# Rotating images by 90 degrees: all loads first, then all stores, on one DMA queue

## The chip, the core and the metric

The kernel runs on one core of a Trainium2 chip. The metric is device time in microseconds (us), the median of several executions. All runs that are compared are on record as fast, with a granted clock of 1.00. Of each kernel one run was profiled.

Some words used below. HBM is the chip's large memory, SBUF the core's own memory of 128 partitions; DMA transfers move data between them, on 16 DMA engines. A transfer has landed when each of its 16 shares has added its step to the transfer's semaphore (the counter that others wait for). An instruction fetch is a packet of the profile's instruction queue (q14).

## The reference

The input is `x` of shape (32, 3, 256, 256) in fp32, 25.17 MB. The output is as large:

```python
def reference(x):
    return np.rot90(x, k=-1, axes=(-2, -1)).astype(np.float32)
```

No arithmetic is done. 25.17 MB must come in from HBM and 25.17 MB must go out.

## The kernel before

The data are cut into 24 slabs of 1 MB. A slab is 128 partitions of 8 rows of 256 numbers, so 8 KB per partition, contiguous in HBM. VectorE's 32x32 transpose, with reversed access patterns, does the rotation. A slab is loaded on the queue of the sync engine (SP), transposed in two halves, and stored on the queue of the scalar engine (ACT).

```python
in_pool = ctx.enter_context(tc.tile_pool(name="in_pool", bufs=12))
out_pool = ctx.enter_context(tc.tile_pool(name="out_pool", bufs=12))
for n in range(n_slabs):                       # 24
    t_in = in_pool.tile([P, R * W], fp32, tag="t_in")      # R = 8, W = 256
    nc.sync.dma_start(out=t_in, in_=ld_v[n])
    t_out = out_pool.tile([P, R * W], fp32, tag="t_out")
    src = t_in.rearrange("p (r g c) -> p c r g", r=R, c=R)
    dst = t_out.rearrange("p (c g r) -> p c r g", c=R, r=R)[:, :, ::-1, ::-1]
    for k in range(PARTS):                     # PARTS = 2
        cs = slice(k * CP, (k + 1) * CP)       # CP = 4
        nc.vector.transpose(out=dst[:, cs], in_=src[:, cs])
    nc.scalar.dma_start(out=st_v[n], in_=t_out,
                        max_dma_last_dim=2048 if n < SHORT else 8192)   # SHORT = 2
# ... (shapes, views and the launch are cut)
```

The first two stores are issued in packets of 2 KB instead of 8 KB.

## Time and profile before

| | before |
|---|---|
| time, median of 6 runs | 124.47 us (124.41 to 124.64) |
| span of the profiled run | 122.8 us |
| VectorE busy | 92.5 us |
| bytes moved | 50.33 MB |

From the page of the kernel before: the busy time of VectorE (DVE); the strip of 40 equal slices with the DMA engines' busy share in tenths and what they moved; the two data queues (packets, MB, share of 16 engines' time); the chain of waits by engine; and VectorE's group.

```profile
span 122.8 us, 186 instructions
...
DVE 92.5 (75%) x48; POOL 0.2 (0%) x4
...
DMA  3999999999999999999999999999999999999993
GB/s 93 422 427 427 393 427 422 415 420 432 426 408 411 427 427 427 427 427 427 427 427 430 427 427 427 427 427 430 427 430 427 427 427 430 424 427 427 427 430 163
...
q1 hardware_dynamic: 3456, 25.17, 49.3%
q10 hardware_dynamic: 4224, 25.17, 48.9%
...
DMA 72%; DVE 8%; DVEq 2%; SPq 1%; issue 0%
...
L54 DVE STREAM_TRANSPOSE t_out<-t_in 128x1024 f32<-128x1024 f32 x48 | 92.5, 2047 | 9.7 <-DMA t_in<-in_x_dram 7.9
```

The DMA strip is full from the second slice to the last but one. VectorE has a quarter of the span to spare. The kernel is bound by the DMA engines.

The table of stretches of the kernel before. The columns are the stretch, its length, the busy time of VectorE and GpSimd with their instruction counts, the clock, the DMA engines' busy share (just over 1 where packets overlap a little), and GB/s.

```profile
core 0: us, DVE busy (x) POOL busy (x), PEclk, DMA share, GB/s
3.00:12.00 9.00, 6.45 (x4) 0.00 (x0) 1.00 1.01 425
12.00:38.00 26.00, 26.00 (x14) 0.00 (x0) 1.00 1.02 417
38.00:62.00 24.00, 24.00 (x14) 0.00 (x0) 1.00 1.01 427
...
64.00:120.00 56.00, 34.09 (x18) 0.00 (x0) 1.00 1.01 427
```

At 3 to 12 us only loads run, from 38 to 97 us loads and stores are mixed, after 98 us only stores are left. The rate to compare with is 427 GB/s. What is below it lies at the start and at 12 to 38 us, in two dips of the rate near 12 and 36 us. A stretch counts a packet where it starts, so up to 16 packets of 8 KB can fall on either side of an edge: over 9 us that is 15 GB/s, over 24 us 5 GB/s. Differences of a few GB/s are safe only in the long stretches.

### The profile page before, as it was taken

The numbers are of one execution on the slowest core, as the hardware profiler recorded it, in microseconds if no ns is written. First come the engines' busy times: TensorE is split into PE (matmuls) and PEld (weight loads), VectorE is DVE, ScalarE is ACT, GpSimd is POOL, SyncE is SP. The second block draws the span as 40 slices with busy tenths as digits, with TensorE's granted clock in tenths as the row PEclk, the third lists the DMA queues.
The fourth block names the chain that finished last, engine by engine and source line by source line (L and its number), as shares of the span: only waits on it lengthen the run. The fifth ranks groups of instructions, "written<-read, shape, count | busy, mean of one in ns | idle before, by whom it ended". The sixth has DMA issues, their size and how long they took to land.

```text
span 122.8 us, 186 instructions
## 1 busy us (share of the span) xinstructions
DVE 92.5 (75%) x48; POOL 0.2 (0%) x4
## 2 busy tenths in 40 slices
DVE  0199999999999999999999999897796693000000
POOL 0000000000000000000000000000000000000000
DMA  3999999999999999999999999999999999999993
GB/s 93 422 427 427 393 427 422 415 420 432 426 408 411 427 427 427 427 427 427 427 427 430 427 427 427 427 427 430 427 430 427 427 427 430 424 427 427 427 430 163
DMA packets 7681, 50.34 MB, mean 410 GB/s; under 512 B 768, under 2 KB 768, under 8 KB 1792
## 3 DMA queue, kind: packets, MB, share of 16 engines
q1 hardware_dynamic: 3456, 25.17, 49.3%
q10 hardware_dynamic: 4224, 25.17, 48.9%
q14 instruction: 1, 0.01, 0.0%
HBM read 25.17 MB, written 25.17 MB: 410 GB/s over the span
## 4 chain that ended last, share of the span: by engine, by line
DMA 72%; DVE 8%; DVEq 2%; SPq 1%; issue 0%
DMA t_in<-in_x_dram 72%; DVE t_out L54 8%; DVEq L83 2%; SPq L47 1%; DVEq L54 0%
## 5 line engine op out<-in xcount | busy, mean ns | idle before, releaser
L54 DVE STREAM_TRANSPOSE t_out<-t_in 128x1024 f32<-128x1024 f32 x48 | 92.5, 2047 | 9.7 <-DMA t_in<-in_x_dram 7.9
L72 POOL MEMSET const-bfloat16-1.0<- 128x1 bf16 x1 | 0.1, 101 | 0.0
L72 POOL MEMSET const-uint8-127<- 128x1 uint8 x1 | 0.1, 101 | 0.0
L72 POOL MEMSET const-float32-0.0<- 128x1 f32 x1 | 0.1, 98 | 0.2 <-issue 0.2
L72 POOL MEMSET const-float32-1.0<- 128x1 f32 x1 | 0.1, 98 | 0.0
## 6 DMA issues: line engine op xcount, KB each, us to landing
t_in<-in_x_dram SPq DMA_DIRECT2D x24, 1024.0 KB, 14.5
out_dram<-t_out ACTq DMA_DIRECT2D x24, 1024.0 KB, 19.5
```

The source lines that it names most:

```text
L47: nc.sync.dma_start(out=t_in, in_=ld_v[n])
L54: nc.vector.transpose(out=dst[:, cs], in_=src[:, cs])
L72: nc = _bacc.Bacc("TRN2", target_bir_lowering=False, num_devices=1)
L83: with _tile.TileContext(nc) as tc:
```

## The change

All loads are issued first, then all stores, and all on SP's queue. With 25 units of 8 KB per partition no load ever waits for a buffer: slab n is transposed into the unit that slab n-1 left, and slab 0 into the spare one. The short rows go. The first store is cut into its first row (1 KB per partition) and the rest.

```diff
-    in_pool = ctx.enter_context(tc.tile_pool(name="in_pool", bufs=12))
-    out_pool = ctx.enter_context(tc.tile_pool(name="out_pool", bufs=12))
+    pools = [ctx.enter_context(tc.tile_pool(name=f"unit{u}", bufs=1)) for u in range(N_UNITS)]
+    units = [p.tile([P, R * W], fp32, name=f"u{u}") for u, p in enumerate(pools)]
     for n in range(n_slabs):
-        t_in = in_pool.tile([P, R * W], fp32, tag="t_in")
-        nc.sync.dma_start(out=t_in, in_=ld_v[n])
+        nc.sync.dma_start(out=units[n], in_=ld_v[n])
-        t_out = out_pool.tile([P, R * W], fp32, tag="t_out")
+    for n in range(n_slabs):
+        t_in, t_out = units[n], units[n - 1]
         # ... the two transposes, the same
-        nc.scalar.dma_start(out=st_v[n], in_=t_out,
-                            max_dma_last_dim=2048 if n < SHORT else 8192)
+        cuts = [0, W, R * W] if n == 0 else [0, R * W]
+        for a, b in zip(cuts, cuts[1:]):
+            nc.sync.dma_start(out=st_v[n][:, a:b], in_=t_out[:, a:b])
```

The intent is a stream of DMA work in which nothing waits for a buffer, with one turn from reading HBM to writing it.

More of the change, by code (lines that the diff above doesn't have):

```diff
@@ L34 @@
     n_slabs = B * C * G // P
-    PARTS = 2
-    SHORT = 2
-    CP = R // PARTS
+    N_UNITS = n_slabs + 1
     ld_v = x.rearrange("b c h w -> (b c h) w").rearrange("(n p r) w -> n p (r w)", p=P, r=R)
     st_v = out.rearrange("b c h w -> (b c h) w").rearrange("(n p c) w -> n p (c w)", p=P, c=R)
-    in_pool = ctx.enter_context(tc.tile_pool(name="in_pool", bufs=12))
-    out_pool = ctx.enter_context(tc.tile_pool(name="out_pool", bufs=12))
+    pools = [ctx.enter_context(tc.tile_pool(name=f"unit{u}", bufs=1)) for u in range(N_UNITS)]
+    units = [p.tile([P, R * W], fp32, name=f"u{u}") for u, p in enumerate(pools)]
     for n in range(n_slabs):
-        t_in = in_pool.tile([P, R * W], fp32, tag="t_in")
-        nc.sync.dma_start(out=t_in, in_=ld_v[n])
-        t_out = out_pool.tile([P, R * W], fp32, tag="t_out")
+        nc.sync.dma_start(out=units[n], in_=ld_v[n])
+    for n in range(n_slabs):
+        t_in, t_out = units[n], units[n - 1]
         src = t_in.rearrange("p (r g c) -> p c r g", r=R, c=R)
         dst = t_out.rearrange("p (c g r) -> p c r g", c=R, r=R)[:, :, ::-1, ::-1]
-        for k in range(PARTS):
-            cs = slice(k * CP, (k + 1) * CP)
+        for h in range(2):
+            cs = slice(h * R // 2, (h + 1) * R // 2)
             nc.vector.transpose(out=dst[:, cs], in_=src[:, cs])
-        nc.scalar.dma_start(out=st_v[n], in_=t_out,
-                            max_dma_last_dim=2048 if n < SHORT else 8192)
+        cuts = [0, W, R * W] if n == 0 else [0, R * W]
+        for a, b in zip(cuts, cuts[1:]):
+            nc.sync.dma_start(out=st_v[n][:, a:b], in_=t_out[:, a:b])
 _INS = ['x']
```

## The prediction

> **What bounds the kernel now.** The DMA engines. It moves 25.17 MB in and 25.17 MB out; the utilisation strip has DMA at nine tenths in every slice but the first and last, and the table of stretches gives 427 GB/s from 38 to 97 us, where loads and stores mix. VectorE is busy 92.5 us of 122.8; the chain of waits is 72% DMA. At 427 GB/s, 50.33 MB take 117.9 us (estimate). The other 4.9 us are, from the same table and the DMA packets: about 2.5 us before the engines run full, about 0.6 us lost between 12 and 38 us (393, 421 and 396 GB/s instead of 427), and about 1.8 us at the end (unequal engines to 121.65 us, then 1.2 us to the end of the span).
>
> **What the change does.**
> 1. Loads and stores no longer mix. This should cost and gain nothing: loads alone run at 425 GB/s (3 to 12 us), the mix at 427, stores alone at 426 (98 to 120 us). The Trainium skill, "DMA: Bandwidth & Descriptors", section "Issuing engines are not separate DMA queues", says that transfers issued by different engines run on the same 16 DMA engines and interleave; the trace agrees.
> 2. The two 2 KB-row stores go. A 2 KB packet took 84 ns, four of them 336 ns, against 309 ns for one 8 KB packet. Two stores are 64 small packets per engine: about 0.4 us. With the dips at 12 and 36 us that is the 0.6 us. A first row of 128 packets of 1 KB is added: under 0.1 us (estimate by the same fixed part per packet).
> 3. One turn from reading to writing, near 61 us. Estimate from the two dips of before: 0.1 to 0.3 us lost.
> 4. Startup and ending are the same.
> 5. The transposes are the same 48, 2.04 us each. No load reuses a unit, so no load waits for VectorE. Slab j is transposed near 5.6 + 3.86(j+1) us, the last at about 98. On the one queue its store can start only after all loads and j stores, at about 61 + 2.46 j us, the last at about 117.6. VectorE is over 15 us ahead everywhere. Stores are issued in order, each also waiting for the transfer eight places earlier; with eight transfers of 2.46 us in flight the engines don't starve.
>
> So only items 2 and 3 lie on the critical path: -0.6 + 0.1 + 0.2 us.
>
> **Prediction.** 124.0 us, 8 in 10 between 123.3 and 125.0. Faster by over 2%: 0.02; within 2%: 0.95; slower by over 2%: 0.03.
>
> **What the profile would show.** Span near 122.3 us. DMA strip full throughout, near 427 GB/s in nearly every slice; one queue, last load landing near 61 us, stores only afterwards, one small dip there. VectorE busy unchanged at 92.5 us, idle from about 98 us to the end for lack of work. The chain of waits almost wholly DMA.
>
> **What would make it wrong.** Reading alone might not hold 425 GB/s for 59 us (before shows only 9 us of it): 4% less would cost 2.4 us. A single queue might drain at the turn, when the stores' first packets wait for the loads' last ones: a bubble of 1 to 2 us. The engines may end more unevenly. The other way, the gain might reach 1 us; more is not there to have.

## The result, and the profile after

The changed kernel took 124.61 us (median of 6, 124.49 to 124.67) against 124.47 us before. A ratio here is always the mean time of one kernel's runs over the mean of the other's in the same rounds, so it is not quite the ratio of the quoted medians. It is 1.0008, with a 95% interval of 0.9995 to 1.0021. The two kernels are equally fast, and the half microsecond that the prediction expected did not come.

The page of the kernel after, the same lines:

```profile
span 122.9 us, 190 instructions
...
DVE 95.6 (78%) x48; POOL 0.2 (0%) x4
...
DMA  3999999999999999999999999999999999999993
GB/s 83 416 427 429 429 424 421 427 427 419 413 419 427 427 421 421 424 424 413 424 414 429 427 429 427 429 429 427 421 427 427 427 429 427 427 427 427 427 435 165
...
q1 hardware_dynamic: 7056, 50.33, 98.0%
q14 instruction: 2, 0.02, 0.0%
...
DVE 43%; issue 34%; DMA 4%; DVEq 2%
...
L53 DVE STREAM_TRANSPOSE u<-u 128x1024 f32<-128x1024 f32 x48 | 95.6, 2057 | 6.4 <-DMA u<-in_x_dram 5.6
```

Two readings need care. First, the chain of waits now names VectorE for 43% and "issue" for 34%. That is not what bounds the kernel. VectorE's last transpose ended at 102.0 us, while the last store landed at 122.05 us; the DMA strip is as full as before. The chain lost the DMA queue because every store here was issued long before its data moved. Second, VectorE's 95.6 us are not slower transposes (2057 ns against 2047 ns). Before, successive transposes overlapped a little, one slab per 3.81 us where nothing else was waited for; now they follow at one slab per 4.02 us, each slab also waiting for VectorE's own previous one. Neither matters.

What the issuing engine waited for, from the view of waits of the kernel after (SPq is SP's sequencer; total us, times, longest us):

```profile
SPq L45 <- DMA u<-in_x_dram: 32.9, 16, 2.2
SPq L57 <- DMA out_dram<-u: 32.7, 17, 2.4
...
SPq L57 <- DMA u<-in_x_dram: 16.7, 8, 2.1
...
SPq L57 <- DVE u L53: 0.6, 2, 0.3
```

Stores hardly ever waited for VectorE (0.6 us). They waited for earlier transfers, as the design wants.

The table of stretches of the kernel after, the same columns:

```profile
3.00:12.00 9.00, 6.32 (x4) 0.00 (x0) 1.00 1.00 422
12.00:38.00 26.00, 25.76 (x14) 0.00 (x0) 1.00 1.01 423
38.00:62.00 24.00, 23.79 (x13) 0.00 (x0) 1.00 1.01 421
...
64.00:120.00 56.00, 37.71 (x19) 0.00 (x0) 1.00 1.01 427
```

At 38 to 62 us before had the mix at 427 GB/s; after has loads alone at 421. From 64 us on, with stores alone, it is back at 427. Between 12 and 38 us after is a little faster than before, and loads alone again.

A finer account comes from the DMA packets of the two traces. For each moment, the time elapsed minus the bytes moved so far divided by 427.5 GB/s is the time lost up to then. Its increase by stretch, in us:

| stretch | before | after | what happens there |
|---|---|---|---|
| 0 to 12 us | 2.61 | 2.70 | start, loads only |
| 12 to 17 | 0.25 | 0.00 | before: the stores begin |
| 17 to 36 | 0.19 | 0.24 | before: 2 KB packets; after: loads only |
| 36 to 38 | 0.22 | 0.02 | before: the stores' packets become 8 KB |
| 38 to 62 | 0.00 | 0.32 | before: the mix; after: loads only |
| 62 to 64 | 0.00 | 0.07 | after: the turn |
| 64 to 121 | 0.10 | 0.05 | |
| sum | 3.37 | 3.40 | |

Before loses 0.66 us from 12 to 38 us, and the change removes nearly all of it. After loses 0.58 us in the loads, all of it from 17 us on, and 0.07 us at the turn. Removing and adding cancel.

How a run of loads loses time shows in the landings (the increments of each transfer's semaphore; the first of its 16) beside the packets:

| after | packets of load done, first engine | landed, first share | lag |
|---|---|---|---|
| load 0 | 5.04 us | 5.38 us | 0.34 us |
| load 3 | 12.41 | 12.81 | 0.40 |
| load 5 | 17.31 | 17.78 | 0.47 |
| load 14 | 39.67 | 40.15 | 0.48 |
| load 23 | 62.02 | 62.50 | 0.48 |

From load 5 to load 23 the landings come every 44.72 / 18 = 2.484 us. Stores 2 to 23 land every (121.31 - 69.82) / 21 = 2.452 us. The packets of the first five loads ran at 2.454 us each, faster than they landed, until they were 0.47 us ahead. Then they were held to the landing rate: 8 KB packets of 309 ns became packets of up to some 321 ns. So the 425 GB/s that the prediction read off the first 9 us of before was the rate of the packets while they ran ahead. The landings of before said otherwise already: loads 0 to 3 landed at 5.23, 7.70, 10.20 and 12.68 us, 2.483 us apart.

### The profile page after: what moved, and what is told of

Same layout as the page of the kernel before. It is cut to its first block, busy times and chain, and to the rows that moved or that the text cites. A ratio compares the mean times of both kernels' runs of the same rounds, so it can differ in the third digit from the quotient of the medians.

```text
span 122.9 us, 190 instructions
## 1 busy us (share of the span) xinstructions
DVE 95.6 (78%) x48; POOL 0.2 (0%) x4
## 4 chain that ended last, share of the span: by engine, by line
DVE 43%; issue 34%; DMA 4%; DVEq 2%
DVE u L53 43%; DMA u<-in_x_dram 4%; DVEq L83 2%
## 5 line engine op out<-in xcount | busy, mean ns | idle before, releaser
L53 DVE STREAM_TRANSPOSE u<-u 128x1024 f32<-128x1024 f32 x48 | 95.6, 2057 | 6.4 <-DMA u<-in_x_dram 5.6
```

## The experiments

Runs of different submissions were on different chips, so they are compared by their ratio to the kernel before, which ran beside each. Two questions were put to the chip. Is the slow run of loads a property of loading, or does VectorE or the queue make it? And are the terms that the change removed (short rows, early turn, the cut row) worth what the reading says?

### e1: before without its short rows

```diff
-    SHORT = 2
+    SHORT = 0
```

> The kernel before with its first two stores in 8 KB rows too, nothing else changed. If the 2 KB rows and the turn that they bring cost what the prediction said, this is 0.4 to 0.6 us faster than before (about 124.0 us) and the load packets' dip at 36 us is gone. Rival: the short rows give the loads priority at the start, and taking them away costs as much as they save; then 124.4 us.

Measured: 124.72 us (before 124.39), ratio 1.0028 (1.0016 to 1.0040): slower, against both expectations. The table of stretches of this run:

```profile
3.00:10.00 7.00, 4.51 (x3) 0.00 (x0) 1.00 1.01 428
10.00:14.00 4.00, 4.00 (x3) 0.00 (x0) 1.00 1.01 346
14.00:20.00 6.00, 6.00 (x4) 0.00 (x0) 1.00 1.02 426
```

The dip moved from 36 us to 10 to 14 us and grew. By the account of lost time it costs 0.82 us from 10 to 17 us (2.49 to 3.31 us), against 0.66 us for the two milder dips and the 2 KB packets of before. The times differ by 0.35 us, the account by 0.16 us, so not all of it is in this one profile. A rival for part of it is the end: an instruction fetch passes at 119.2 us, and the 16 landings of the last store are 1.00 us apart (0.67 for the store before it; 0.85 for the last store of before). What is shown is that the short rows gained nothing by going, and that in this profile the turn without them costs 0.16 us more than with them. The prediction's item 2 had the right sum for what goes away, but only because the change takes away the early turn as well.

### e2: after without VectorE

Each slab is stored from the unit it was loaded into; the result is wrong.

```diff
-        t_in, t_out = units[n], units[n - 1]
+        t_in, t_out = units[n], units[n]
-        for h in range(2):
-            cs = slice(h * R // 2, (h + 1) * R // 2)
-            nc.vector.transpose(out=dst[:, cs], in_=src[:, cs])
```

> The kernel after without the transposes: each slab is stored from the unit it was loaded into (wrong result on purpose). Theory 1: a long run of loads alone lands one slab per 2.484 us, against 2.45 us for a store, whatever VectorE does. Then the loads' landing step stays 2.48 us, and the time stays within 0.2 us of after. Theory 2: VectorE's reads and writes of SBUF slow the loads' writes. Then the step falls to 2.45 us, the last load lands near 62.1 us instead of 62.8, and the time falls by 0.6 to 0.8 us.

Measured: 124.10 us, ratio 0.9977. The table of stretches of this run (VectorE has no column, as it did nothing):

```profile
core 0: us, POOL busy (x), PEclk, DMA share, GB/s
...
17.00:62.00 45.00, 0.00 (x0) 1.00 1.01 422
64.00:120.00 56.00, 0.00 (x0) 1.00 1.01 428
```

The loads land every (62.25 - 17.54) / 18 = 2.484 us, as in after. Theory 2, that VectorE's traffic slows the loads' writes, falls. The Trainium skill, "SBUF — State Buffer", section "SBUF: two separate sides", says that a DMA cannot be slowed by a compute operation; this run agrees.

The time did fall by about 0.4 us against after, which neither theory had, so the reason had to be found. In after, an 8 KB instruction fetch passes at 86.3 us; one data packet there takes 662 ns instead of 309, and the landings of a store, 0.45 us apart from first to last of 16 until then, are 0.79 us apart afterwards. Without the transposes there is no such packet, and the last store landed at 121.61 us instead of 122.05. Of these 0.44 us, some 0.25 are that the last of the 16 landings is nearer to their mean (0.27 us behind it instead of 0.52), which the fetch can explain; the other 0.2 us are that all of them landed earlier, which it does not explain (0.10 us of that was there at 12 us). e6 tests the fetch.

### e3: after with its first store whole

```diff
-        cuts = [0, W, R * W] if n == 0 else [0, R * W]
+        cuts = [0, R * W]
```

> The kernel after with the first store whole instead of one 1 KB row and the rest. By the packet times (46 ns for 1 KB, 272 ns for 7 KB, against 309 ns for 8 KB) the cut costs 8 x 9 ns, so under 0.1 us: the same as after within 0.1 us. If the small row is there to soften the turn from loads to stores and does so, the turn's dip at 62 us (402 GB/s) deepens and the time rises by 0.1 to 0.3 us.

Measured: 124.99 us, ratio 1.0052 (1.0040 to 1.0064). The cut row is worth about 0.5 us by the two ratios to before, far more than expected either way (the two profiled spans differ by 0.30 us). But it is not worth it at the turn: without the cut nothing at all is lost from 62 to 64 us (after: 0.07 us, which is what the cut's packets were estimated to cost, 8 x 9 ns), and the last store landed earlier, at 121.88 us instead of 122.05. What is longer is the end, from the last landing to the end of the span: 1.29 us against 0.82 us. The issuing engine stands still for 0.40 us between two of its last instructions, and an 8 KB instruction fetch comes only then, at 123.0 us. In after that fetch passes at 121.25 us, while the engine still waits for the last stores.

### e4: loads and stores in turn on the one queue

```diff
-    for n in range(n_slabs):
+    LEAD = 4
+    for n in range(LEAD):
         nc.sync.dma_start(out=units[n], in_=ld_v[n])
 ...      # whole stores, and after each of them:
+        if n + LEAD < n_slabs:
+            nc.sync.dma_start(out=units[n + LEAD], in_=ld_v[n + LEAD])
```

> The kernel after with four loads, then store and load in turn on the one queue, no cut row. Theory 1 (only a long run of loads alone is slow; loads between stores are not): a pair of load and store takes 4.906 us, so the slow part, 18 loads x 0.032 us = 0.6 us, goes; about 124.0 us, span about 122.3. If the loads are slow whoever runs between them, or if turns between reading and writing cost 0.01 us or more each, 124.6 us or more.

Measured: 125.29 us (124.55 to 126.17), ratio 1.0076. The expectation failed, but the trace shows its first half was right. The table of stretches of this run:

```profile
3.00:10.00 7.00, 4.42 (x3) 0.00 (x0) 1.00 1.02 430
10.00:14.00 4.00, 3.97 (x3) 0.00 (x0) 1.00 0.95 356
14.00:20.00 6.00, 5.97 (x4) 0.00 (x0) 1.00 1.02 425
```

After 20 us the lost time grows by only 0.1 us until 60 us (3.20 to 3.29): loads between stores are not slow. What spoils it is the early turn, 0.62 us lost from 10 to 14 us, and a few packets of 488 to 835 ns that hold up one engine at a time (at 51.9, 61.4 and 71.1 us, for example). The landings of the last store are 1.85 us apart, so the kernel ends when the slowest engine ends, at 122.89 us.

### e5: the cut at another store

```diff
-        cuts = [0, W, R * W] if n == 0 else [0, R * W]
+        cuts = [0, W, R * W] if n == 12 else [0, R * W]
```

> The kernel after with the first store whole and the thirteenth store cut at its first row instead. In the run with no cut at all the end of the issuing engine's program halted 0.41 us between two of its last instructions and an 8 KB instruction fetch came after it; with the cut that fetch came before the end. Theory 1: the cut helps only because one more instruction shifts where the instruction fetch falls. Then this is as fast as after (ratio to before near 1.001) and has no halt. Theory 2: the small first row softens the turn from loads to stores. Then this is as slow as the run with no cut (ratio near 1.005).

Measured: 124.72 us, ratio 1.0017 (1.0003 to 1.0030). This is as after, not as e3. The fetch passes at 121.21 us and there is no halt. The first row alone at the thirteenth store does the same as at the first, so it has nothing to do with the turn. The turn itself, from 62 to 64 us, again lost next to nothing (0.01 us): the 0.05 us turned up near 92 us instead, where the cut store now lies. So the 0.05 to 0.07 us of after, e2, e6 and e10 at 62 us are the cut row's, not the turn's.

### e6: one transpose per slab in the kernel after

```diff
-        for h in range(2):
-            cs = slice(h * R // 2, (h + 1) * R // 2)
-            nc.vector.transpose(out=dst[:, cs], in_=src[:, cs])
+        nc.vector.transpose(out=dst, in_=src)
```

> The kernel after with one transpose of a whole slab instead of two of half a slab; the DMAs are the same. If the 0.34 us by which the 16 engines' landings spread apart at 86 us comes from the 8 KB instruction fetch there, and that fetch is for VectorE's instructions, 24 fewer of them remove it or move it, the spread of the last stores falls from 0.65-0.75 us to 0.45 us or less, and the time falls by about 0.3 us, ratio to before near 0.998. If the fetch is for the issuing engine, nothing changes: ratio 1.001.

Measured: 124.74 us, ratio 1.0018. The mechanism was as expected: no fetch at 86 us, landings of the last store 0.42 us apart, and the last landing at 121.47 us, 0.58 us earlier than in after. Some 0.35 us of that are the last landing's distance from the mean of the 16 (0.17 us instead of 0.52); the rest is again that all landed earlier, for reasons not found. The gain was given back at the end: the issuing engine halted for 0.42 us and the end took 1.29 us, as in e3. Here the time did not move although the transfers ended earlier.

The end of the span in the traces, in us:

```
kernel   last landing   end of span   between   instruction fetches during the run
before      122.00        122.82       0.81     106.6
after       122.05        122.87       0.82     86.3, 121.3
e1          122.15        122.96       0.81     119.2
e2          121.61        122.33       0.72     none
e3          121.88        123.17       1.29     86.2, 123.0
e4          122.89        123.83       0.94     102.4, 124.1
e5          122.07        122.89       0.82     86.0, 121.2
e6          121.47        122.76       1.29     122.5
e7          121.84        122.82       0.98     none
e8          122.67        123.39       0.72     none
e9          122.05        123.34       1.29     91.6, 123.2
e10         121.86        123.14       1.28     122.9
e11         121.81        122.62       0.81     none
e12         121.86        122.68       0.82     86.0, 120.8
```

Apart from e4 and e7 the end takes 0.72 to 0.82 us or 1.28 to 1.29 us. The longer one goes with a fetch that comes after the last landing; e4 has such a fetch too (after the end of its span), and an end between the two. (e7 has another reason, told there.) That the halt of 0.40 to 0.42 us and the late fetch belong together is seen in every run but e4; that one causes the other is not shown.

### e7: loads of 2 MB

This is e2 with 12 loads of two slabs each (wrong result).

```diff
-    for n in range(n_slabs):
-        nc.sync.dma_start(out=units[n], in_=ld_v[n])
+    for m in range(n_slabs // 2):
+        nc.sync.dma_start(out=pairs[m], in_=ld2_v[m])
 ...      # the tiles of two slabs and their views are cut here
```

> The run without VectorE (wrong result on purpose) with 12 loads of 2 MB, the same 8 KB packets, instead of 24 of 1 MB. If the loads lose 0.032 us per transfer (its completion), a 2 MB load lands every 4.93 us and the last load lands 0.3 us earlier than in that run, near 62.4 us. If they lose it per packet or byte, 4.97 us and no change.

Measured: 124.58 us, ratio 1.0008. The table of stretches of this run:

```profile
17.00:62.00 45.00, 0.00 (x0) 1.00 1.01 422
64.00:120.00 56.00, 0.00 (x0) 1.00 1.01 428
```

A 2 MB load lands every (62.53 - 17.79) / 9 = 4.971 us. The loss goes with packets or bytes, not with the transfers' completions. (Its span is 0.49 us longer than e2's for other reasons: 0.22 us were lost in the first loads, and the end took 0.26 us more, because the issuing engine asked for the last transfer's semaphore first and then for four others.)

### e8: the same writes without reading HBM

This is e2 with loads 3 to 23 replaced by copies from unit 0 in SBUF (wrong result).

```diff
-        nc.sync.dma_start(out=units[n], in_=ld_v[n])
+        nc.sync.dma_start(out=units[n], in_=ld_v[n] if n < 3 else units[0])
```

> The run without VectorE with all but the first three loads replaced by copies from the first loaded unit in SBUF into the units (wrong result on purpose), so HBM isn't read after 13 us. If writing SBUF is what holds a run of loads to one slab per 2.484 us, the copies take 2.48 us each too. If reading HBM does, they take 2.45 us or less each.

Measured: 125.35 us, ratio 1.0066. The table of stretches of this run:

```profile
8.00:14.00 6.00, 0.00 (x0) 1.00 0.99 367
17.00:62.00 45.00, 0.00 (x0) 1.00 1.01 423
64.00:120.00 56.00, 0.00 (x0) 1.00 1.01 426
```

The copies land every (63.01 - 15.81) / 19 = 2.484 us, the same as the loads. HBM is not read in that time, so reading HBM is not what holds the loads back. What loads and copies share is that they write SBUF. (That the copies are held to the same step by some other cause is unlikely, but no run excludes it.) The run is slower because the turn from loads to copies, before 14 us, cost 0.90 us (lost time 2.54 us at 6 us, 3.44 us at 14 us).

### e9: eight loads ahead instead of four

```diff
-    LEAD = 4
+    LEAD = 8
```

> The alternating order on one queue with eight loads ahead instead of four, so that the first store's data follow at about 22 us and not at 12.6. Theory 1: the 0.6 us that the four-load version lost between 10.8 and 13 us comes from the first store reaching the engines while they are still reading ahead of what has landed; after some 17 us of loads alone (reads held back by the landing rate) the turn costs under 0.1 us, as it did at 62 us in after. Then no long load packets at 11 us, about 0.15 us lost on the loads, and up to 0.6 us less than the four-load version. Theory 2: the loss comes with the issue of the first store at 9.6 us; then the dip stays at 11 us. In either case single engines may fall behind one by one, as in the four-load version (spread of the landings 1.9 us at the end), which would keep it slower than before.

Measured: 125.31 us, ratio 1.0065. The table of stretches of this run:

```profile
10.00:14.00 4.00, 3.97 (x3) 0.00 (x0) 1.00 1.02 430
14.00:20.00 6.00, 5.97 (x4) 0.00 (x0) 1.00 1.01 421
20.00:24.00 4.00, 3.97 (x3) 0.00 (x0) 1.00 0.93 334
24.00:60.00 36.00, 35.69 (x19) 0.00 (x0) 1.00 1.01 428
```

The dip moved with the first store's data to 20 to 24 us, so theory 2 (the issue at 9.6 us causes it) falls. But it costs 0.87 us there, although the packets had run fully ahead, so theory 1 falls as well. From 30 to 86 us, with loads and stores in turn, the lost time grows by 0.01 us.

### e10: one transpose per slab, and two cut stores

```diff
-        cuts = [0, W, R * W] if n == 0 else [0, R * W]
+        cuts = [0, W, R * W] if n in (0, 12) else [0, R * W]
 ...      # and one transpose per slab, as in e6
```

> The version of after with one transpose per slab had its last landing at 121.47 us (after: 122.05) but halted 0.44 us at the end and gained nothing. Here the thirteenth store is cut as well, one more instruction on the issuing engine. If that instruction again moves the instruction fetch out of the end, there is no halt, the last landing is near 121.5 us and the span near 122.4: ratio to before near 0.998. If halt and early landing don't combine so, ratio 1.001 to 1.002.

Measured: 124.87 us, ratio 1.0020. The end halted again (1.28 us), and the early landing did not come either: the last store landed at 121.86 us, not near 121.5. There is no fetch at 86 us, but the 16 landings of a store went from 0.49 to 0.71 us apart where the second cut store lies, near 92 us. One more instruction on the issuing engine does not reliably move the fetch, so the simple rule behind this run is wrong. That the halt goes with a late fetch still holds; what decides when the fetch comes is open.

### e11: one transpose per slab in the kernel before

```diff
-    PARTS = 2
+    PARTS = 1
```

> The kernel before with one transpose per slab. If its instruction fetch at 106.6 us is for VectorE and costs its engine 0.35 us (spread of the landings from 0.53 to 0.96 us there), the fetch goes and the last landing comes 0.35 us earlier: ratio 0.997, unless the end halts instead, then 1.000. Longer transposes delay the first store by nothing, since it waited for the whole slab before too.

Measured: 124.40 us, ratio 0.9988 (0.9974 to 1.0002). The fetch is gone and the end does not halt. The last of the 16 final landings is 0.31 us behind their mean instead of 0.60, so what the fetch cost is gained. But the last landing came only 0.19 us earlier: in this run the dip at 36 us cost 0.35 us instead of 0.22. It is the fastest correct version, and not clearly faster than before.

### e12: one load behind the first store

```diff
-    for n in range(n_slabs):
+    for n in range(n_slabs - 1):
         nc.sync.dma_start(out=units[n], in_=ld_v[n])
 ...      # after the first slab's two stores:
+        if n == 0:
+            nc.sync.dma_start(out=units[n_slabs - 1], in_=ld_v[n_slabs - 1])
```

> The kernel after with the last load moved behind the first slab's store, nothing else. The turn from loads to stores cost 0.07 us in after, where no load follows, and 0.5 to 0.9 us in the two alternating runs and in before without its short rows, where loads follow or run beside. Theory 1: the loss at the turn comes from loads that follow the first store. Then the packets of the load ahead of it lengthen near 58 to 60 us, 0.5 us or more is lost there, and the ratio to before rises to 1.005 or more. Theory 2: the turn is cheap because it comes late, or because the queue is full, whatever follows. Then no more than 0.15 us is lost there and the ratio stays within 1.000 to 1.003.

Measured: 124.67 us, ratio 1.0023 (1.0007 to 1.0039). From 60 to 64 us 0.05 us was lost. That speaks against theory 1 and fits theory 2. It is not conclusive: this run kept the small cut row between the loads and the next large store, as the runs with a costly turn did not.

## Why the prediction was right in its range and wrong in its sum

The measured 124.61 us lies in the range and in the class foretold, 0.6 us above the predicted 124.0. That says little for the reasoning: the range of 123.3 to 125.0 also holds no change at all, and the result stayed near before because a gain that was foreseen met a loss of about the same size that was not. The prediction's sum for the critical path was -0.6 + 0.1 + 0.2 us (that is -0.3 us; its 124.0 us lies 0.5 below before).

1. **"Loads no longer mix. This should cost and gain nothing: loads alone run at 425 GB/s."** This is the step that failed. Loads alone land one slab per 2.484 us against 2.452 us for stores, and the run of 18 such loads from load 5 on costs 18 x 0.032 = 0.58 us. The account of lost time has the same 0.58 us for 17 to 62 us. e2, e7 and e8 show that VectorE, the number of transfers and the reading of HBM are not the cause; SBUF as the target of the writes is what is left, by elimination. e4 and e9 show that loads placed between stores don't lose it. The prediction named the risk ("Reading alone might not hold 425 GB/s") but read the size from packets that ran ahead, not from landings.
2. **Removing the short rows and the dips gains 0.6 us.** Right in size: 0.66 us lost from 12 to 38 us before, 0.26 us after, all of it the slow loads. The reason was partly wrong: e1 shows that removing the short rows alone makes the early turn dearer. What gains is that the early turn goes.
3. **One turn costs 0.1 to 0.3 us.** It cost 0.07 us with the cut row and next to nothing without it (e3, e5), so the estimate from the dips of before was too high. It lies at 62 us, where it was put within 2 us. The cut row goes with another gain: with it the instruction fetch comes before the end and the end is 0.47 us shorter (after, e5, against e3). With one transpose per slab it does not help (e6, e10).
4. **Start and end are the same.** Measured 0.81 and 0.82 us at the end, and the start within 0.09 us. But the end is the same only with the cut row; without it, it is 0.47 us longer.
5. **VectorE is far off the path.** Right in effect, though a slab took 4.02 us instead of 3.86, so VectorE ended at 102.0 and not about 98 us. The chain of waits was not "almost wholly DMA"; in this kernel it is a poor witness.

So the sum as measured is -0.66 (items 2) + 0.58 (loads alone) + 0.07 (turn with its cut row) + 0.09 (start, within the scatter of the profiles) - 0.05 (later) = +0.03 us, and the profiled spans differ by 0.06 us.

What stays open: why the turn at 62 us costs next to nothing, and the turn at 10 to 24 us (8 to 14 us in e8) 0.6 to 0.9 us, whether the following work writes HBM (e1, e4, e9) or SBUF (e8). Loads behind the store don't make it dear in e12, but the cut row was there. Also open is why a long run of transfers into SBUF is 1.3% slower than one out of it, and what decides when an instruction fetch comes.

## What to carry to other kernels

When the DMA engines bound a kernel, read the sustained rate from landings, not from the packets of the first microseconds, which can run ahead. Reordering transfers trades one small loss for another here: ask what each kind of transfer costs alone, mixed, and at the turn. At a level of half a microsecond, the number of instructions and the place of their fetches count as much as the transfers, so test a small trick (such as a cut row) at another place before explaining it.

## What the Trainium skill lacked or had wrong

- "DMA: Bandwidth & Descriptors", section "Where 436 GB/s comes from", gives the SBUF ports one ceiling, 435.2 GB/s, and does not tell transfers into SBUF from those out of it. In these runs a long run of transfers into SBUF landed 1 MB every 2.484 us (422 GB/s), one from SBUF to HBM every 2.452 us (428 GB/s), and loads and stores mixed ran at 427 GB/s.
- No page has the cost of a turn from loads to transfers that read SBUF: none to 0.07 us at 62 us, 0.6 to 0.9 us at 10 to 24 us; with 2 KB packets 0.66 us in two dips, against 0.82 us without (before against e1).
- "Runtime: NRT & Kernel Launch", section "Instruction fetch mechanics", says that the sequencer fetches its next instructions over its own DMA queue and that this is mostly hidden. Here, in after, the 16 landings of a store were 0.45 us apart before an 8 KB fetch and 0.79 us after it (still 0.64 us before the second fetch, 35 us later), and a fetch that fell into the end went with a halt that made the end 0.47 us longer (e3).
